# Feed-forward weights at other distances from their moving operand, and three raw weight buffers instead of four

## The chip, the cores and the metric

The kernel runs on one core of one Trainium2 chip. The metric is the device time of one execution in microseconds. The engines are TensorE (PE, with its weight loads shown apart as PEld), VectorE (DVE), ScalarE (ACT), GpSimd (POOL) and SyncE (SP, which here issues the weight DMAs).

## The reference

A trunk of four residual layers over 256 tokens of width 1024, in float32. Each layer adds a token mixer (layer 0 and 3 a Mamba-2 SSD, layer 1 an HGRN2 recurrence, layer 2 a gated DeltaNet), then cross-attention into 256 memory tokens, then a gated feed-forward block; a final RMSNorm follows. The part that the change is about:

```python
D_MODEL = 1024; SEQ = 256; DEPTH = 4; D_FF = 2816
...
def conv_glu_ffn(h, up_w, conv_w, conv_b, down_w):
    gate, up = jnp.split(h @ up_w, 2, axis=-1)
    gate = causal_dwconv(gate, conv_w) + conv_b
    return (jax.nn.silu(gate) * up) @ down_w
...
    for i in range(DEPTH):
        hn = rmsnorm(x, ln_mix[i])
        # mixer i % 3: mamba2, hgrn2, gated_deltanet
        x = x + mix
        x = x + memory_cross_attention(rmsnorm(x, ln_xattn[i]), rmsnorm(mem, ln_mem[i]), xa_q[i], xa_kv[i], xa_o[i])
        x = x + conv_glu_ffn(rmsnorm(x, ln_ffn[i]), f_up[i], f_conv_w[i], f_conv_b[i], f_down[i])
    return rmsnorm(x, final_norm)
```

## The kernel before

All activations stay on the chip with the feature on the partition and the 256 tokens along the row. Every weight matrix streams in once, in tiles of 128 x 1024 float32 (512 KB). `prep` (L152) makes one such tile ready: a DMA on SP's queue fills `raw`, ScalarE casts it to the rounded format float32r as `wH` (L160), VectorE subtracts the two to get the rest `wL` (L161). There are four `raw`, three `wH` and three `wL` buffers. `mm3` (L166) then multiplies in three matmuls: wH by the activations' high part (L168), wH by their low part (L169), wL by the high part (L170). In all of them the weights' 128 x 128 block is the stationary operand, loaded by an LDWEIGHTS before its matmul, and 256 columns of activations are the moving one; only in `proj_tok` and in the second half of `mem_kv` is it the other way round.

`proj` (L229) uses one weight tile for 8 k-tiles x 3 matmuls; its moving operand is `hH` or `hL`. `out_proj` (L254) walks groups of four k-tiles and uses a tile for 2 column blocks x 4 k-tiles x 3; its moving operand is `aH` or `aL`. `ffn` (L453) calls `proj` 22 times with two tiles each (`f_up`, 1056 matmuls a layer, into `ffps`), and then `out_proj` for `f_down` (528 matmuls a layer, into `acc`), which has 22 k-tiles in six groups. `mem_kv` before the next layer's mixer has 384 matmuls.

The order of work is the scheduler's: weight tiles are made under a raised priority, so they run as far ahead as buffers allow, and `Weave` mixes the steps of the mixers' heads in between the weight matmuls. Each engine and SP's queue take their instructions in order.

Addresses matter for what follows. In the built program a partition's row of SBUF holds `hH` from byte 20672, `hL` from 28864, `wH` from 80896, 84992 and 89088, `wL` from 93184, 97280 and 101376, `aH` and `aL` from 105664 to 120000 in steps of 2048, and `mH` and `mL` (the split memory tokens) from 131264 and 139456. All `hH`, `hL`, `aH`, `aL`, `mH`, `mL` rows begin 192 bytes past a multiple of 512, all `wH` and `wL` rows on one, and the blocks within a tile are multiples of 512 bytes apart. So between a moving operand and the weights that are loaded meanwhile the distance, moving minus stationary, is 192 bytes modulo 512 (320 where the roles are exchanged). A few others exist: in the attention scores keys move and queries stand, both 192 past a multiple, so the distance is 0; the Mamba dt projection has 32 columns of weights for each k-tile, so its weights start 128 bytes further each time.

Of the kernel before, what the change touches and what calls it, by code (L numbers as in the profile page):

```python
# [9 lines left out]
F32R = mybir.dt.float32r  # L10
# [6 lines left out]
P = 128  # L17
D = 1024
T = 256
# [3 lines left out]
NFF = 22  # L23
# [63 lines left out]
def tile_trunk(ctx: ExitStack, tc: tile.TileContext, io: dict, out: bass.AP, layers=range(DEPTH), parts="mxf", final=True):  # L87
    nc = tc.nc
    ACT, DVE, POOL, PE = nc.scalar, nc.vector, nc.gpsimd, nc.tensor
    weave = Weave()  # L90
    WB = [4,3,3]
    HL = [607, 282, 1973, 470, 14335, 1000]
    NL = [9214]
    LAT = [21000, 5620, 1450, 1042, 1588, 1117, 1724, 2353, 942, 2058, 8335, 1093, 4452, 2125, 1556]
# [6 lines left out]
    wp = ctx.enter_context(tc.tile_pool(name="wp", bufs=3))  # L101
# [6 lines left out]
    def phase(name, bufs=1):  # L108
        return tc.tile_pool(name=name, bufs=bufs, reuse_waits="tile")
# [4 lines left out]
    def bank(name):  # L114
        return ps_acc.tile([P, 512], F32, tag="acc", name=name)

    def flat(ap):
        return ap.rearrange("p a b -> p (a b)")

    def pcol(name, i):  # L120
        o = PO[name] + i
        return prm[:, o:o + 1]

    def f32(ap):
        return ap.bitcast(F32)
# [23 lines left out]

    between = []  # L150

    def prep(src, n=1024, step=1024):  # L152
        with tc.high_priority(offset=PRIO):
            raw = wp.tile([P, 1024], F32, tag="raw", name="raw", bufs=WB[0])
            H = wp.tile([P, 1024], F32R, tag="wH", name="wH", bufs=WB[1])
            L = wp.tile([P, 1024], F32R, tag="wL", name="wL", bufs=WB[2])
            for o in range(0, n, step):
                c = slice(o, min(n, o + step))
                nc.sync.dma_start(out=raw[:, c], in_=src[:, c])
                ACT.copy(H[:, c], raw[:, c])  # L160
                DVE.tensor_tensor(out=L[:, c], in0=raw[:, c], in1=f32(H[:, c]), op=ALU.subtract)  # L161
                if len(between) > 1:
                    between[-1](between.pop(0))
        return H, L

    def mm3(dst, aH, aL, bH, bL, start, stop):  # L166

        PE.matmul(dst, aH, bH, start=start, stop=False, skip_group_check=True)  # L168
        PE.matmul(dst, aH, bL, start=False, stop=False, skip_group_check=True)  # L169
        PE.matmul(dst, aL, bH, start=False, stop=stop, skip_group_check=True)  # L170

    def split(src, H, L):
        return (ACT.copy(H, src), DVE.tensor_tensor(out=L, in0=src, in1=f32(H), op=ALU.subtract))  # L173

# [5 lines left out]

    def split_gain(src, g, H, L):

        ACT.activation(out=H, in_=src, func=AF.Copy, scale=g)  # L183
        DVE.scalar_tensor_tensor(out=L, in0=src, scalar=g, in1=f32(H), op0=ALU.mult, op1=ALU.subtract)  # L184


    def exp_ln_tables(*after):

        i = ACT.preload_act_table_set("natural_log_exp_and_others")
        behind([i] * len(after), after)  # L190
# [35 lines left out]
        yield 440, 0  # L226


    def proj(srcs, ps):  # L229

        for i, s in enumerate(srcs):
            H, L = prep(s)
            for kt in range(KT):
                c = slice(kt * P, (kt + 1) * P)
                mm3(ps[:, i * T:(i + 1) * T], H[:, c], L[:, c], hH[:, kt, :], hL[:, kt, :],
                    i == 0 and kt == 0, kt == KT - 1)
                if kt % 2:
                    weave.tick(654)
# [12 lines left out]
                    if k % 2:  # L251
                        weave.tick(654)

    def out_proj(wsrc, nk, a, gens=None, gname=None, layer=0, last=False):  # L254


        accs = [bank(f"acc{b}") for b in range(4)]
        ng = (nk + 3) // 4
        st = Stats(DVE if last else POOL)
        for g in range(ng):  # L260
            n = min(4, nk - 4 * g)
            if gens is not None:
                weave.finish(gens[g])
            aH, aL = [], []
            for k in range(0, n, 2):
                H = ap_.tile([P, 2, T], F32R, tag="aH", name="aH")
                L = ap_.tile([P, 2, T], F32R, tag="aL", name="aL")
                split(a[:, 4 * g + k:4 * g + k + 2, :], H, L)
                aH += [H[:, 0, :], H[:, 1, :]]
                aL += [L[:, 0, :], L[:, 1, :]]  # L270
            for b in range(4):
                H, L = prep(wsrc[g, b], n * T)
                for cb in range(2):
                    for k in range(n):
                        kt = 4 * g + k
                        c = slice(k * T + cb * P, k * T + (cb + 1) * P)
                        mm3(accs[b][:, cb * T:(cb + 1) * T], H[:, c], L[:, c], aH[k], aL[k],
                            kt == 0 and cb == 0, kt == nk - 1)
                        if k % 2:
                            weave.tick(654)  # L280
                if g == ng - 1:
                    xs = flat(xT[:, 2 * b:2 * b + 2, :])
                    DVE.tensor_tensor(out=xs, in0=xs, in1=accs[b], op=ALU.add)
                    if gname is not None:
                        for kt in (2 * b, 2 * b + 1):
                            split_gain(xT[:, kt, :], pcol(gname, layer * 8 + kt), hH[:, kt, :], hL[:, kt, :])
                    st.add(xs)
                    if last:
                        for kt in (2 * b, 2 * b + 1):
                            fg = pcol("final", kt)  # L290
                            if b < 3:
                                POOL.tensor_scalar(out=KTt[:, kt, :], in0=xT[:, kt, :], scalar1=fg, scalar2=None, op0=ALU.mult)
                            else:
                                ACT.activation(out=KTt[:, kt, :], in_=xT[:, kt, :], func=AF.Copy, scale=fg)
        return st

    def conv(c, src, wcol, width, bias):

        if bias is None:
            ACT.activation(out=c, in_=src, func=AF.Copy, scale=wcol(width - 1))  # L300
        else:
            ACT.activation(out=c, in_=src, func=AF.Identity, scale=wcol(width - 1), bias=bias)
        for j in range(1, width):
            DVE.scalar_tensor_tensor(out=c[:, j:], in0=src[:, :T - j], scalar=wcol(width - 1 - j), in1=c[:, j:],
                                     op0=ALU.mult, op1=ALU.add)
# [80 lines left out]
    def attention(layer, st):  # L386
        with ExitStack() as ex:
# [46 lines left out]
            for h in range(4):  # L434
# [12 lines left out]
                if h < 3:  # L447
                    behind(split(KTt[:, 2 * h + 2:2 * h + 4, :], *kvs[h + 1][0]), sp)
                gens.append(weave.push(late(AL[2], head(h, qH, qL))))
            return out_proj(io["xa_o"][layer], KT, oT, [gens[:2], gens[2:]], "ln_ffn" if "f" in parts else None, layer)  # L450

    def late(ns, gen):
# [4 lines left out]
    def ffn(layer, st, hook=None, last=False):  # L457
        with ExitStack() as ex:
            wk = ex.enter_context(phase(f"ff{layer}", 2))
            aT = wk.tile([P, NFF, T], F32, name="aT", bufs=1)  # L460
            rs = np_.tile([P, T], F32, tag="nrs", name="nrs", bufs=1)
            def gate(t, ps):
                gu = wk.tile([P, 2, T], F32, tag="gu", name="gu")
                DVE.tensor_tensor(out=gu, in0=ps.rearrange("p (a b) -> p a b", a=2),
                                  in1=rs.unsqueeze(1).to_broadcast([P, 2, T]), op=ALU.mult)
                c = wk.tile([P, T], F32, tag="c", name="c")
                conv(c, gu[:, 0, :], lambda j: pcol("f_cw", (layer * NFF + t) * 3 + j), 3, pcol("f_cb", layer * NFF + t))
                silu = ACT.activation(out=c, in_=c, func=AF.Silu)
                DVE.tensor_tensor(out=aT[:, t, :], in0=c, in1=gu[:, 1, :], op=ALU.mult)
                return silu  # L470

            todo = []
            for t in range(NFF):
                ps = bank("ffps")
                proj([io["f_up"][layer, 2 * t + i] for i in range(2)], ps)
                todo.append((t, ps))
                if t == 0:
                    continue
                if t == 1:
                    st.rs(rs)  # L480
                for u in todo:
                    silu = gate(*u)
                todo = []
                if t == 6 and hook is not None:
                    hook(silu)
            exp_ln_tables(silu)
            return out_proj(io["f_down"][layer], NFF, aT, last=last)

    def softplus(u, n, tmp):

# [669 lines left out]
    for i, l in enumerate(layers):  # L1160
# [7 lines left out]
        else:  # L1168
            for kt in range(KT):
                g = "ln_xattn" if "x" in parts else "ln_ffn"  # L1170
# [13 lines left out]
    for b in range(4):  # L1184
        o = Vt.rearrange("p a (b t) -> p (a b) t", t=T)[:, 2 * b:2 * b + 2, :]
# [125 lines left out]
```

## Time and profile before

| | us |
|---|---|
| median of two runs (2066.68 and 2073.19) | 2069.93 |
| the profiled execution | 2072.47 |
| its span, first to last instruction | 2070.7 |
| TensorE busy in it | 2025.5 |
| VectorE busy | 1590.6 |
| ScalarE busy | 1282.5 |
| mean granted TensorE clock, share of full | 0.997 |

A matmul is counted as busy from its start to a modelled end, and the next one starts before that end. So the busy time says that TensorE hardly stops, and the time of one matmul is read from start to start.

### The profile page before, as it was taken

To read this page: it belongs to the slowest core of one execution; us is meant where nothing else is said; L and a number is where in the kernel's file an instruction comes from. 1 tells how busy PE (TensorE), PEld (TensorE's weight loads), DVE (VectorE), ACT (ScalarE), POOL (GpSimd) and SP (SyncE) were. 2 spreads that over 40 slices of the span, in tenths; PEclk is the share of its full clock that TensorE was granted. 3 is DMA by queue.
4 is the path that set the end of the run, shared out by engine and by line. 5 is a ranking of instruction groups with operands and counts; after the bars stand their busy time and mean duration, and the time that the engine had idled before them with its cause. 6 is when DMAs were issued, how large, how long until landed. Compare 5 with 4: busy or idle time off the path is not lost.

```text
span 2070.7 us, 42162 instructions
## 1 busy us (share of the span) xinstructions
PE 2025.5 (98%) x17084; PEld 1971.5 (95%) x17084; DVE 1590.6 (77%) x2423; ACT 1282.5 (62%) x1874; POOL 344.5 (17%) x468
## 2 busy tenths in 40 slices
PE   8999999999999999999999999999999999999997
PEld 8999999999999899999988889999999999999997
DVE  6899787875688777866786775778757999778765
ACT  6677666654565566555676875666545777666553
POOL 2032211000132110001064451110000223201001
PEclk9999999999999999999999999999999999999999
DMA  7554555655654446666543333456656444545663
GB/s 239 163 155 152 162 154 162 206 188 170 206 157 140 149 137 195 203 195 192 186 130 126 114 113 115 139 163 211 195 179 196 151 154 150 174 133 183 186 189 115
DMA packets 110372, 343.10 MB, mean 166 GB/s; under 512 B 15456, under 2 KB 25312, under 8 KB 110176
## 3 DMA queue, kind: packets, MB, share of 16 engines
q1 hardware_dynamic: 106176, 333.42, 52.0%
q10 hardware_dynamic: 3744, 6.71, 1.0%
q8 instruction: 134, 2.20, 0.4%
q0 software_dynamic: 256, 0.26, 0.1%
q14 instruction: 62, 0.51, 0.1%
HBM read 336.42 MB, written 3.93 MB: 164 GB/s over the span
## 4 chain that ended last, share of the span: by engine, by line
PE 79%; DVE 6%; issue 5%; ACT 4%; DMA 3%; POOL 2%; ACTq 0%; SPq 0%; DVEq 0%; POOLq 0%
PE acc L168 7%; PE ffps L170 7%; PE acc L169 7%; PE ffps L169 7%; PE ffps L168 7%; PE acc L170 7%; PE mps L168 4%; PE mps L169 4%; PE mps L170 4%; DVE wL L161 2%; PE kvps L170 2%; PE kvps L168 2%; PE kvps L169 2%; PE qps L170 2%; PE qps L168 2%
## 5 line engine op out<-in xcount | busy, mean ns | idle before, releaser
L161 DVE TENSOR_TENSOR wL<-raw,wH 128x1024 fp32r<-128x1024 f32 (+2 forms) x639 | 776.1, 1216 | 318.9 <-ACT wH L160 316.6
L160 ACT CAST wH<-raw 128x1024 fp32r<-128x1024 f32 (+2 forms) x639 | 658.4, 1031 | 510.6 <-PE ffps L169 156.4
L168 PE MATMUL acc<-aH,wH 128*128 128x256 f32 x1408 | 396.4, 282 | 0.6 <-ACT aH L173 0.6
L170 PE MATMUL ffps<-hH,wL 128*128 128x256 f32 x1408 | 392.6, 279 | 1.8 <-DVE wL L161 1.7
L168 PE MATMUL ffps<-hH,wH 128*128 128x256 f32 x1408 | 392.0, 279 | 2.5 <-ACT hH L183 2.5
L170 PE MATMUL acc<-aH,wL 128*128 128x256 f32 x1408 | 393.0, 279 | 0.0
L169 PE MATMUL acc<-aL,wH 128*128 128x256 f32 x1408 | 392.4, 279 | 0.1
L169 PE MATMUL ffps<-hL,wH 128*128 128x256 f32 x1408 | 392.1, 279 | 0.2
L168 PEld LDWEIGHTS ffps<-hH,wH 128*128 128x128 f32 x1408 | 265.5, 189 | 3.4 <-ACT hH L183 3.3
L168 PEld LDWEIGHTS acc<-aH,wH 128*128 128x128 f32 x1408 | 265.2, 189 | 3.5 <-issue 1.3
L170 PEld LDWEIGHTS ffps<-hH,wL 128*128 128x128 f32 x1408 | 264.4, 188 | 4.1 <-DVE wL L161 3.7
L169 PEld LDWEIGHTS acc<-aL,wH 128*128 128x128 f32 x1408 | 265.6, 189 | 1.5 <-issue 0.5
L169 PEld LDWEIGHTS ffps<-hL,wH 128*128 128x128 f32 x1408 | 265.1, 188 | 1.1 <-DVE hL L184 0.6
L170 PEld LDWEIGHTS acc<-aH,wL 128*128 128x128 f32 x1408 | 264.6, 188 | 0.4 <-DVE wL L161 0.2
L168 PE MATMUL mps<-hH,wH 128*128 128x256 f32 x768 | 219.8, 286 | 0.0
L170 PE MATMUL mps<-hH,wL 128*128 128x256 f32 x768 | 215.0, 280 | 0.0
L169 PE MATMUL mps<-hL,wH 128*128 128x256 f32 x768 | 214.9, 280 | 0.0
L203 POOL TENSOR_TENSOR ns<-nsq 128x256 f32<-128x256 f32 x13 | 10.5, 811 | 856.5 <-ACT nsq L200 856.5
L168 PEld LDWEIGHTS mps<-hH,wH 128*128 128x128 f32 x768 | 145.1, 189 | 2.7 <-issue 2.4
L170 PEld LDWEIGHTS mps<-hH,wL 128*128 128x128 f32 x768 | 145.4, 189 | 0.1
L169 PEld LDWEIGHTS mps<-hL,wH 128*128 128x128 f32 x768 | 144.5, 188 | 0.3
L170 PE MATMUL gps<-hH,wL 128*128 128x256 f32 x448 | 127.2, 284 | 0.9 <-DVE wL L161 0.9
(397 smaller groups left out, 4489.9 us busy)
## 6 DMA issues: line engine op xcount, KB each, us to landing
raw<-f_up SPq DMA_DIRECT2D x176, 512.0 KB, 3.6
raw<-m_in SPq DMA_DIRECT2D x96, 512.0 KB, 3.5
raw<-f_down SPq DMA_DIRECT2D x80, 512.0 KB, 3.5
raw<-xa_kv SPq DMA_DIRECT2D x60, 512.0 KB, 4.2
raw<-g_in SPq DMA_DIRECT2D x48, 512.0 KB, 3.9
raw<-m_out SPq DMA_DIRECT2D x32, 512.0 KB, 3.5
raw<-xa_q SPq DMA_DIRECT2D x32, 512.0 KB, 3.5
raw<-xa_o SPq DMA_DIRECT2D x32, 512.0 KB, 3.5
```

The source lines that it names most:

```text
L160: ACT.copy(H[:, c], raw[:, c])
L161: DVE.tensor_tensor(out=L[:, c], in0=raw[:, c], in1=f32(H[:, c]), op=ALU.subtract)
L168: PE.matmul(dst, aH, bH, start=start, stop=False, skip_group_check=True)
L169: PE.matmul(dst, aH, bL, start=False, stop=False, skip_group_check=True)
L170: PE.matmul(dst, aL, bH, start=False, stop=stop, skip_group_check=True)
L203: self.eng.tensor_tensor(out=self.sum, in0=sq[:, :T], in1=sq[:, T:], op=ALU.add)
```

## The change

`prep` takes a parameter `far`, the distance in bytes modulo 512 from the weights to their moving operand. Its `wH` and `wL` buffers are 1152 instead of 1024 columns wide, and the tile uses 1024 of them from an offset of (192 - far) modulo 512 bytes. All callers keep 192, except the feed-forward block: f_up has one distance for its first eleven `proj` calls and another for the last eleven, f_down one for its first three groups (288 matmuls) and another for the last three (240), and both tables differ by layer. To make room for the six wider buffers, `raw` has three buffers instead of four.

```diff
-    WB = [4,3,3]
+    WB = [3,3,3]
...
-    def prep(src, n=1024, step=1024):
+
+    FAR = 192
+    UP = [(64, 96), (224, 256), (384, 416), (128, 288)]
+    DOWN = [(128, 160), (288, 352), (448, 192), (256, 384)]
+
+    def prep(src, n=1024, step=1024, far=FAR):
+        o = (FAR - far) % 512 // 4
         with tc.high_priority(offset=PRIO):
             raw = wp.tile([P, 1024], F32, tag="raw", name="raw", bufs=WB[0])
-            H = wp.tile([P, 1024], F32R, tag="wH", name="wH", bufs=WB[1])
-            L = wp.tile([P, 1024], F32R, tag="wL", name="wL", bufs=WB[2])
+            H = wp.tile([P, 1152], F32R, tag="wH", name="wH", bufs=WB[1])[:, o:o + 1024]
+            L = wp.tile([P, 1152], F32R, tag="wL", name="wL", bufs=WB[2])[:, o:o + 1024]
...
-    def proj(srcs, ps):
+    def proj(srcs, ps, far=FAR):
...
-            H, L = prep(s)
+            H, L = prep(s, far=far)
...
-    def out_proj(wsrc, nk, a, gens=None, gname=None, layer=0, last=False):
+    def out_proj(wsrc, nk, a, gens=None, gname=None, layer=0, last=False, fars=(FAR, FAR)):
...
-                H, L = prep(wsrc[g, b], n * T)
+                H, L = prep(wsrc[g, b], n * T, far=fars[2 * g // ng])
...
-                proj([io["f_up"][layer, 2 * t + i] for i in range(2)], ps)
+                proj([io["f_up"][layer, 2 * t + i] for i in range(2)], ps, UP[layer][2 * t // NFF])
...
-            return out_proj(io["f_down"][layer], NFF, aT, last=last)
+            return out_proj(io["f_down"][layer], NFF, aT, last=last, fars=DOWN[layer])
```

TensorE's instructions in the feed-forward layers stand in the same order before and after. With one raw buffer fewer the scheduler moves some others: single casts, subtractions and residual sums at the end of two of the f_down's, and many steps in layer 2's mixer. On SP's queue, in the first heads of layer 2's mixer (`raw<-g_in` are weight tiles; `gd<-MT`, `blk<-gd` and `U<-gd` carry a head's matrix out to memory and back), there stood before:

```order
L159 DMA raw<-g_in 128x1024
L928 DMA blk<-gd_12483 32x16x16
L159 DMA raw<-g_in 128x1024 x4
L958 DMA U<-gd_12485 128x4x128
L159 DMA raw<-g_in 128x1024
L927 DMA gd_12484<-MT 128x4x128
L928 DMA blk<-gd_12484 32x16x16
L159 DMA raw<-g_in 128x1024 x3
```

and now (the lines are six higher):

```order
L165 DMA raw<-g_in 128x1024
L934 DMA blk<-gd_12483 32x16x16
L165 DMA raw<-g_in 128x1024 x3
L964 DMA U<-gd_12485 128x4x128
L165 DMA raw<-g_in 128x1024
L933 DMA gd_12484<-MT 128x4x128
L165 DMA raw<-g_in 128x1024
L934 DMA blk<-gd_12484 32x16x16
L165 DMA raw<-g_in 128x1024 x3
```

Three weight tiles instead of four stand between the first head's `blk` and its `U`, and the one left over stands between the second head's `gd` and `blk`.

On VectorE, in the same heads (`kq`, `kd`, `gqd`, `MT` and `gatt` are steps of a head, `gc` the convolution that empties a weight product's bank `gps`), there stood before:

```order
L889 TENSOR_TENSOR kq<-qk,grs 128x2x128
L890 SCALAR_TENSOR_TENSOR kq<-qk,grs 128x2x128
L946 TENSOR_TENSOR kd<-er,kq 128x256
L947 TENSOR_TENSOR gqd<-er,kq 128x256
L919 SCALAR_TENSOR_TENSOR MT<-E,gtcol,gp 128x128 x3
L304 SCALAR_TENSOR_TENSOR gc_12853<-gps,prm,gc_12853 128x255
L919 SCALAR_TENSOR_TENSOR MT<-E,gtcol,gp 128x128
L304 SCALAR_TENSOR_TENSOR gc_12853<-gps,prm,gc_12853 128x254
L161 TENSOR_TENSOR wL<-raw,wH 128x1024
L304 SCALAR_TENSOR_TENSOR gc_12853<-gps,prm,gc_12853 128x253
```

and now:

```order
L895 TENSOR_TENSOR kq<-qk,grs 128x2x128
L896 SCALAR_TENSOR_TENSOR kq<-qk,grs 128x2x128
L310 SCALAR_TENSOR_TENSOR gc_12853<-gps,prm,gc_12853 128x255
L952 TENSOR_TENSOR kd<-er,kq 128x256
L310 SCALAR_TENSOR_TENSOR gc_12853<-gps,prm,gc_12853 128x254
L925 SCALAR_TENSOR_TENSOR MT<-E,gtcol,gp 128x128
L310 SCALAR_TENSOR_TENSOR gc_12853<-gps,prm,gc_12853 128x253
L925 SCALAR_TENSOR_TENSOR MT<-E,gtcol,gp 128x128 x3
L167 TENSOR_TENSOR wL<-raw,wH 128x1024
```

The three steps of the convolution now stand ahead of most of `MT`, and `gqd` comes later.

## Rows read from the trace of the kernel before

**Rows 1.** The page: the span, TensorE's busy time and count, and the engines' shares of the chain that ended last.

```profile
span 2070.7 us, 42162 instructions
...
PE 2025.5 (98%) x17084; PEld 1971.5 (95%) x17084; DVE 1590.6 (77%) x2423; ACT 1282.5 (62%) x1874; POOL 344.5 (17%) x468
...
PE 79%; DVE 6%; issue 5%; ACT 4%; DMA 3%; POOL 2%; ACTq 0%; SPq 0%; DVEq 0%; POOLq 0%
```

**Rows 2.** The waits of TensorE, longest first in total: who waited for whom, us in total, times, longest.

```profile
PE kvps L168 <- ACT wH L160: 7.0, 1, 7.0
PE grp L1035 <- ACT S L1030: 3.6, 2, 1.8
...
PE ffps L170 <- DVE wL L161: 1.7, 5, 0.5
...
PE gps L170 <- DVE wL L161: 0.9, 2, 0.6
```

**Rows 3.** Windows in the feed-forward layers, TensorE alone: the window (us from the start of the span), its length, TensorE's busy time and the matmuls that touch the window, the granted clock, the DMA engines' share, GB/s. In order: layer 0 first half of f_up, then second half with f_down; layers 1 and 2 the same; layer 3 from the first half of f_up to the end of f_down.

```profile
348.00:385.00 37.00, 37.00 (x329) 1.00 0.65 208
400.00:519.00 119.00, 119.00 (x1013) 1.00 0.59 185
785.00:820.00 35.00, 35.00 (x312) 1.00 0.65 205
835.00:951.00 116.00, 116.00 (x1026) 1.00 0.65 192
1383.00:1420.00 37.00, 37.00 (x328) 1.00 0.65 206
1433.00:1549.00 116.00, 116.00 (x1026) 1.00 0.62 192
1886.00:2058.00 172.00, 172.00 (x1462) 1.00 0.56 172
```

**Rows 4.** Groups by line in two of these windows, 835 to 951 us (first row) and 1886 to 2058 us (second): busy us and mean ns of one, idle before.

```profile
L169 PE MATMUL ffps<-hL,wH 128*128 128x256 f32 x171 | 47.2, 276 | 0.0
...
L169 PE MATMUL ffps<-hL,wH 128*128 128x256 f32 x315 | 88.5, 281 | 0.0
```

**Rows 5.** TensorE in order of time around 396 us, in layer 0's f_up: start us, duration us, line and names.

```profile
395.52 0.28 PE L168 MATMUL ffps<-hH,wH 128*128 128x256 f32 x1
395.63 0.28 PE L169 MATMUL ffps<-hL,wH 128*128 128x256 f32 x1
396.37 0.39 PE L170 MATMUL ffps<-hH,wL 128*128 128x256 f32 x1 [0.45 <-DVE wL L161]
...
396.94 0.28 PE L168 MATMUL ffps<-hH,wH 128*128 128x256 f32 x1
```

**Rows 6.** The page's costliest groups: of f_up's matmuls the first and the last of three lines.

```profile
L170 PE MATMUL ffps<-hH,wL 128*128 128x256 f32 x1408 | 392.6, 279 | 1.8 <-DVE wL L161 1.7
...
L169 PE MATMUL ffps<-hL,wH 128*128 128x256 f32 x1408 | 392.1, 279 | 0.2
```

**Rows 7.** TensorE in order of time in the attention scores of layer 1's second head: the first two and the last of twelve matmuls in a row.

```profile
729.62 0.28 PE L168 MATMUL sc<-k1H,qH 128*128 128x256 f32 x1
729.74 0.28 PE L169 MATMUL sc<-k1L,qH 128*128 128x256 f32 x1
...
730.94 0.28 PE L170 MATMUL sc<-k1H,qL 128*128 128x256 f32 x1
```

**Rows 8.** Windows in mem_kv of layer 1 and of layer 2, TensorE alone, columns as in rows 3.

```profile
535.00:564.00 29.00, 29.00 (x248) 1.00 0.61 182
970.00:994.00 24.00, 24.00 (x214) 1.00 0.60 183
```

**Rows 9.** TensorE in order of time in layer 0's dt projection: the first and the last of eighteen matmuls in a row.

```profile
57.32 0.28 PE L168 MATMUL dtps<-hH,wH 128*32 128x256 f32 x1
...
59.25 0.28 PE L170 MATMUL dtps<-hH,wL 128*32 128x256 f32 x1
```

**Rows 10.** Making weight tiles in layer 1's f_up: DMA issues (count, KB each, median us to landing), then SP's queue, VectorE and ScalarE in order of time.

```profile
raw<-f_up SPq DMA_DIRECT2D x176, 512.0 KB, 3.6
...
843.80 16.53 SPq L159 DMA_DIRECT2D raw<-f_up  x7
...
842.56 1.22 DVE L161 TENSOR_TENSOR wL<-raw,wH 128x1024 fp32r<-128x1024 f32 x1
...
844.07 1.05 ACT L160 CAST wH<-raw 128x1024 fp32r<-128x1024 f32 x1 [0.92 <-PE ffps L169]
...
852.23 1.05 ACT L160 CAST wH<-raw 128x1024 fp32r<-128x1024 f32 x1 [1.17 <-PE ffps L169]
```

**Rows 11.** Layer 2's mixer in order of time: SP's queue, ScalarE, TensorE.

```profile
1062.99 2.16 SPq L159 DMA_DIRECT2D raw<-g_in  x3
1081.31 0.38 SPq L958 DMA_DIRECT2D U<-gd  x1
1081.79 0.45 SPq L159 DMA_DIRECT2D raw<-g_in  x1
...
1087.34 2.05 SPq L159 DMA_DIRECT2D raw<-g_in  x4
...
1086.10 1.04 ACT L160 CAST wH<-raw 128x1024 fp32r<-128x1024 f32 x1 [3.25 <-DMA raw<-g_in]
...
1087.41 0.36 ACT L1030 COPY S<-gs 128x256 f32<-128x256 f32 x1
...
1087.83 0.71 PE L1035 MATMUL grp<-S,kd 128*128 128x128 f32 x4 [1.82 <-ACT S L1030]
```

**Rows 12.** The window of layer 2's mixer with its output projection: length, busy us and instructions of TensorE, its weight loads, VectorE, ScalarE and GpSimd, clock, DMA share, GB/s.

```profile
999.00:1316.00 317.00, 301.72 (x2441) 284.18 (x2440) 235.18 (x441) 223.10 (x334) 121.88 (x271) 0.99 0.41 130
```

## The prediction, made before the changed kernel ran

> **What bounds the kernel now.** I read the page's first lines, then TensorE's waits, then the feed-forward stretches one by one. TensorE is busy 2025.5 of 2070.7 us, in 17084 matmuls, and holds 79% of the chain that ended last [rows 1]. The 45.2 us in which it is idle are many small waits: the longest, 7.0 us, is the start; behind it come waits of 2 to 4 us in total each, none on a weight tile in the feed-forward layers worth more than 2 us [rows 2]. So the time is the number of matmuls times the distance from one start to the next, and that step is what to look at.
>
> A row of the windows view counts every matmul that touches the window, so the step is (window + one duration) / count. In the feed-forward stretches with no wait it takes just two values [rows 3, 4]: (37 + 0.28)/329 = 113.3 ns in the first half of layer 0's f_up, 119.28/1013 = 117.8 ns from there to the end of its f_down; 113.3 ns in all of layer 1 and layer 2 (116.28/1026); 117.8 ns in all of layer 3 (172.28/1462). The duration moves with it, 276 against 281 ns. The granted clock is 1.00, the 2.4 GHz level, in all seven, so this is no clock effect. The program, the shapes and the 192 bytes are the same in all these stretches; what differs is how the stream started. At 396 us TensorE waits 0.45 us for wL, and the steps are 113 ns before and 118 ns after, up to 520 us [rows 3, 5]. I read that as a stream of moving reads and the load of the next weights getting in each other's way by one of two fixed amounts, set at each restart and kept until the next.
>
> **The change part by part.**
>
> *The distance.* f_up and f_down run 4 x (1056 + 528) = 6336 matmuls: 1408 on each of mm3's three lines for ffps, 4224 in all [rows 6], and 528 per layer in f_down (22 k-tiles x 8 column blocks x 3). No instruction is added or moved there; only the address of the stationary operand slides by up to 480 bytes. Before, 3696 of them (528 of layer 0, 1584 each of layers 1 and 2) step at 113.3 and 2640 at 117.8 ns: 418.8 + 311.0 = 729.8 us, a mean of 115.2 ns. After, fifteen of the sixteen sections have a distance that f_up and f_down have not had, so the cost is bounded from the nearest rows:
> - At 0 bytes (the attention scores, keys moving, queries stationary) eleven steps in a row from 729.62 to 730.94 us make 120 ns [rows 7]. All at 120 ns: 6336 x 4.8 ns = +30.4 us.
> - At 320 bytes (the second half of mem_kv, weights and activations with their roles exchanged, and the first half at 192) both values occur: 118.1 ns at 535 us, 113.4 ns at 970 us [rows 8]. So a distance need not choose between the two.
> - The small dt projection has 32 weight columns per k-tile, so its weights start 128 bytes further each time and the distance runs through 192, 64, 448 and 320. It steps at (59.25 - 57.32)/17 = 113.5 ns [rows 9]: the better value stands at four distances, and even a short weight load doesn't go under it. I take 113.3 ns for the floor. All there: 6336 x -1.9 ns = -12.0 us.
>
> I take the middle, 116.7 ns: distances such as 224, 288 and 352 lie next to the two whose rows show either value (mean 115.5), 64, 96, 416 and 448 between these and the 120 ns at zero. That is 6336 x 1.5 ns = **+9.5 us**, between -12 and +30.
>
> Here the Trainium skill speaks for another result. "TensorE: Matmul & The Clock Gate", Part 2 (step by step, LDWEIGHTS), says that TensorE reads SBUF through two independent ports, one for the moving operand and one for the weight load, and that loading the next weights takes no read bandwidth from the running matmul. By that the distance would be worth nothing, and the term 0. The trace doesn't bear it out fully: the step is 113.3, 117.8 or 120 ns for one shape at one clock [rows 3, 7].
>
> *Three raw buffers.* A weight tile's DMA is issued when VectorE has subtracted the tile four (now three) places ahead. In f_up seven issues take 16.5 us, 2.7 us apart, and each follows at once on a subtraction: it ends at 843.78, the DMA that refills the buffer goes at 843.80 and that tile is cast at 852.23 [rows 10], 8.4 us later. Landing takes 3.6 us in the median, so some 4.8 us are spare; with three buffers the issue moves one tile, 2.7 us, later, and about 2 us stay. ScalarE waits there for TensorE to release wH, not for the DMA [rows 10], and three wH tiles are 8 us of matmuls ahead. Cost there: 0. If that cover were gone, each late tile would cost its lateness, below 1 us.
>
> The place where it can cost is layer 2's mixer, the gated delta net. There SP's queue also carries the head's transfers: the DMA of U waits until 1081.31, and the raw tiles queued behind it go at 1081.79 and 1087.34, after three at 1063 [rows 11]. So what is loaded before such a block is all that TensorE has; ScalarE waits 3.25 us for a raw tile at 1086, the copy of S is queued behind that cast at 1087.41, and TensorE waits 1.82 us for S [rows 11]. The new order of SP's queue has one raw tile fewer ahead of U in the first head and takes the raw loads apart around blk later. For each of the eight heads one tile less is ready. There is room: for a weight tile itself TensorE waits in this stage 0.9 us in all, on two occasions [rows 2]. I bound the buffers' part by 0 and four heads that wait as this one did, 4 x 1.8 = 7 us. The scheduler also puts the conv steps of VectorE in another place among the head's steps; I bound that by a quarter, either way, of the 15.3 us for which TensorE idles in this stage (317 - 301.7) [rows 12], so -4 to +11 together. I take **+2 us**, about the one wait that a row shows.
>
> *The rest.* All other weights keep 192 bytes. Their streams may restart on the other value after a feed-forward layer; 384 matmuls of the next mem_kv are 1.7 us each way, and I take 0.
>
> *The sum.* The profiled execution took 2072.47 us (span 2070.7): 2072.5 + 9.5 + 2 = 2084. It lies 2.5 us over the median of the runs, 2069.93, so the forecast for the median is 2069.9 + 11.5 = **2081 us**.
>
> **The rivals.**
> 1. *The distance does nothing; each section falls on 113.3 or 117.8 by its restart.* For: the two values at one distance, and the skill's rule above. Against: 120 ns at zero [rows 7]. If the sections draw evenly, 115.5 ns, 6336 x 0.3 = +2, with the +2 of the buffers 2074 us; that all the sections that ran at 117.8 fall on it again gives 2072.
> 2. *192 is a poor place and most others sit on the floor.* For: layers 0 and 3 paid 117.8 for 2640 matmuls, and the dt projection ran at 113.5 through four distances. Against: with 32 columns its weight load is a quarter as long. It gives -12 + 2: 2060 us. More than 2% faster would need 108.7 ns a step, below anything that 256 columns with a weight load show here.
> 3. *Some distances make the weight load and the moving reads collide all the way, and 120 isn't the worst.* Place: those sections of f_up and f_down whose distance meets the delay between the two reads. It decides from a mean of 115.2 + 41.4/6.336 = 121.7 ns on. If half of the matmuls went at 130, 3168 x 14.8 = +47 us: 2119 us. For: zero bytes need not be the worst, since the two reads don't start together by anything the trace shows. Against: no stretch without a wait, at any distance in this trace, steps at more than 121 ns.
> 4. *The raw buffers starve TensorE.* If the spare 2 us were eaten, 272 feed-forward tiles would be late by under 1 us each, and the wH tiles hide that first; only if the delta-net waits all came, +9 on top of the +2 of the forecast, 2090 us: still no change by 2%.
>
> **How the numbers follow.** 2% of 2070 is 41 us, about what a measurement of this kernel can tell from no change. The forecast (a mean step between 115.7 and 120 ns, 2073 to 2110 us) gets 0.61, rival 1 0.14, rival 2 0.10, rival 3 0.10, rival 4 beside the others 0.05. Low end: -12 for the floor and -2 in the delta net, 2056. High end: +30 and +8 of the delta net's +11, 2108; beyond it lie rival 3 and little else. Faster by over 2% 0.02, within 0.87, slower 0.11 (rival 3, and a little of the forecast's upper end with the delta net).
>
> **What would show it.** In the windows of each half of f_up and f_down, the step should be one steady value per section, none under 113, most between 113.3 and 120; the same values for the two sections that share a distance (128, 256, 288, 384) would prove the distance, different ones rival 1. A section over 125 ns without waits is rival 3. ScalarE's waits for raw tiles should grow in the delta net alone. Wrong I would be if the mixers, whose distance stays, moved by more than 10 us.

## The result, and the profile after

The changed kernel takes 2090.77 us in the median of two runs (2089.07 and 2092.46) against 2069.93: a ratio of 1.0104, 95% interval 1.0073 to 1.0135. That is a loss of 1.0%, less than the 2% that one comparison can tell. The interval comes from two runs of each kernel and says little of the kernel before's own spread: in the later comparisons its 43 runs lie between 2057.24 and 2083.09 us, all below both runs here. So the loss is there, but its size is less sure than the interval says. The profiled execution took 2092.46 us. Its page, against [rows 1]:

```profile
span 2090.7 us, 42161 instructions
...
PE 2044.1 (98%) x17084; PEld 1991.0 (95%) x17084; DVE 1590.3 (76%) x2423; ACT 1282.5 (61%) x1875; POOL 342.5 (16%) x468
...
PE 85%; issue 5%; DVE 5%; ACT 4%; DMA 1%; POOL 1%; DVEq 0%; ACTq 0%; SPq 0%; POOLq 0%
```

TensorE is busy 18.6 us longer with the same 17084 matmuls; the span is 20.0 us longer. So on balance the time went into longer steps; TensorE's waits grew in one stage and shrank in others. The windows of the sixteen sections, TensorE alone, columns as in [rows 3], in the order first and second half of f_up, first and second half of f_down, layers 0 to 3:

```profile
348.00:385.00 37.00, 37.00 (x316) 1.00 0.63 201
400.00:455.00 55.00, 55.00 (x461) 1.00 0.62 194
464.00:491.00 27.00, 27.00 (x229) 1.00 0.58 181
497.00:519.00 22.00, 22.00 (x187) 1.00 0.48 149
790.00:820.00 30.00, 30.00 (x256) 1.00 0.57 179
845.00:897.00 52.00, 52.00 (x436) 1.00 0.62 193
905.00:933.00 28.00, 28.00 (x242) 1.00 0.59 189
938.00:960.00 22.00, 22.00 (x186) 1.00 0.47 143
1400.00:1440.00 40.00, 40.00 (x340) 1.00 0.60 194
1450.00:1505.00 55.00, 55.00 (x472) 1.00 0.64 200
1511.00:1538.00 27.00, 27.00 (x241) 1.00 0.60 194
1543.00:1565.00 22.00, 22.00 (x197) 1.00 0.48 156
1905.00:1950.00 45.00, 45.00 (x378) 1.00 0.58 182
1957.00:2012.00 55.00, 55.00 (x474) 1.00 0.59 188
2018.00:2047.00 29.00, 29.00 (x244) 1.00 0.58 184
2053.00:2075.00 22.00, 22.00 (x187) 1.00 0.37 120
```

By the prediction's formula, (window + 0.28)/count, each row gives its section's step, to about 0.5 ns for the short ones. The table is sharper: it has the mean step over all starts of TensorE in the section that follow one another without a wait.

| layer | f_up 1 | f_up 2 | f_down 1 | f_down 2 |
|---|---|---|---|---|
| 0 | 64: 117.6 ns | 96: 120.0 | 128: 118.7 | 160: 118.7 |
| 1 | 224: 118.3 | 256: 120.0 | 288: 116.7 | 352: 120.0 |
| 2 | 384: 118.7 | 416: 117.3 | 448: 113.4 | 192: 113.3 |
| 3 | 128: 119.8 | 288: 116.7 | 256: 120.0 | 384: 118.7 |

The clock is 1.00, 2.4 GHz, in every row, as before. Weighted by its matmuls the table gives 748.7 us, 118.2 ns a step, where [rows 3] gave 729.8.

By the starts of the stages, from one stage's first matmul to the next one's, f_up gained 2.4, 4.7, 3.5 and 0.4 us in layers 0 to 3 and f_down (the last one with the final norm) 0.5, 2.6, 0.0 and 1.3: +15.4 in the feed-forward. Layer 2's mixer gained 4.5; the other stages come to 0.1 together, with +1.7 and -1.6 in the attention of layers 1 and 2 among them. The stages show 3.5 us less than the 18.9 of the steps, because waits shrank: TensorE's 1.7 us for wL in f_up [rows 2] are gone, which fits longer steps that give VectorE more time. The rest was not traced to a wait.

In layer 2's mixer the window that answers to [rows 12], all engines:

```profile
1010.50:1332.00 321.50, 302.35 (x2455) 284.85 (x2454) 236.98 (x442) 224.60 (x337) 119.72 (x271) 0.98 0.42 129
```

TensorE idles 321.5 - 302.35 = 19.2 us instead of 15.3. Its wait for gsq in this window, and ScalarE's for raw tiles, first in the kernel before and then in the changed one, where the first is TensorE's longest:

```profile
PE l L883 <- ACT gsq L880: 0.7, 2, 0.4
...
ACT wH L160 <- DMA raw<-g_in: 6.5, 2, 3.3
```

```profile
PE l L889 <- ACT gsq L886: 8.9, 2, 8.7
...
ACT wH L166 <- DMA raw<-g_in: 12.3, 3, 8.8
```

The wait for gsq, a ScalarE step of a head, grew from 0.7 to 8.9 us. The one for S, 3.6 us in [rows 2], is gone, and others have shrunk: so 8.2 us more of this wait made only 3.9 us more idle time. Where it comes from, in order of time, SP's queue and then ScalarE, beside [rows 11]:

```profile
1051.91 4.83 SPq L165 DMA_DIRECT2D raw<-g_in  x3
1069.83 0.38 SPq L964 DMA_DIRECT2D U<-gd  x1
1070.30 0.46 SPq L165 DMA_DIRECT2D raw<-g_in  x1
...
1075.95 1.04 ACT L166 CAST wH<-raw 128x1024 fp32r<-128x1024 f32 x1 [8.77 <-DMA raw<-g_in]
...
1078.84 0.63 ACT L886 ACTIVATE gsq<-qk 128x512 f32<-128x512 f32 x1
```

SP's queue stands at the head's U until 1069.83. The raw tile behind it goes at 1070.30 and lands some 5.6 us later. ScalarE's cast waits 8.77 us for it, and gsq, which needs no weight, is queued behind that cast.

The wait has a tail. Two windows of TensorE alone, the wait and the time soon after it, and the first and last of nine matmuls in a row in the second:

```profile
1071.00:1079.50 8.50, 0.00 (x0) 0.71 0.76 224
1082.50:1085.00 2.50, 2.50 (x14) 0.53 0.00 0
```

```profile
1082.89 0.41 PE L174 MATMUL gps<-hH,wH 128*128 128x256 f32 x1
...
1084.59 0.40 PE L176 MATMUL gps<-hH,wL 128*128 128x256 f32 x1
```

While TensorE waits, its granted clock falls from 1.00 to 0.50, the 1.2 GHz level, and it is back at 1.00 only at some 1084.8 us: these matmuls step at (1084.59 - 1082.89)/8 = 212 ns instead of 113 to 118.

### The profile page after: what moved, and what is told of

It is laid out like the page before. It is cut to its first block, busy times and chain, and to the rows that moved or that the text cites. A ratio compares the mean times of both kernels' runs of the same rounds, so it can differ in the third digit from the quotient of the medians.

```text
span 2090.7 us, 42161 instructions
## 1 busy us (share of the span) xinstructions
PE 2044.1 (98%) x17084; PEld 1991.0 (95%) x17084; DVE 1590.3 (76%) x2423; ACT 1282.5 (61%) x1875; POOL 342.5 (16%) x468
## 4 chain that ended last, share of the span: by engine, by line
PE 85%; issue 5%; DVE 5%; ACT 4%; DMA 1%; POOL 1%; DVEq 0%; ACTq 0%; SPq 0%; POOLq 0%
PE ffps L176 8%; PE ffps L174 8%; PE ffps L175 8%; PE acc L174 7%; PE acc L175 7%; PE acc L176 7%; PE mps L174 4%; PE mps L175 3%; PE mps L176 3%; PE kvps L176 2%; PE kvps L174 2%; PE kvps L175 2%; DVE wL L167 2%; PE qps L176 2%; PE qps L175 2%
## 5 line engine op out<-in xcount | busy, mean ns | idle before, releaser
L174 PE MATMUL ffps<-hH,wH 128*128 128x256 f32 x1408 | 396.5, 282 | 2.5 <-ACT hH L189 2.5
L175 PE MATMUL ffps<-hL,wH 128*128 128x256 f32 x1408 | 396.6, 282 | 0.1
```

## The experiments

Two things were to be settled: whether the distance itself sets the step, or each section merely draws a value when its stream restarts (when TensorE takes up its matmuls again after a wait); and whether the mixer pays for the missing raw buffer. In e1 to e4, e6 and e7 the diffs are against the changed kernel, in e5, e8 and e9 against the kernel before.

**e1: three raw buffers, everything at 192.**

```diff
-    UP = [(64, 96), (224, 256), (384, 416), (128, 288)]
-    DOWN = [(128, 160), (288, 352), (448, 192), (256, 384)]
+    UP = [(192, 192), (192, 192), (192, 192), (192, 192)]
+    DOWN = [(192, 192), (192, 192), (192, 192), (192, 192)]
```

> The changed kernel with every distance back at 192: three raw buffers and the wider wH and wL alone. If the distances made the feed-forward layers slower, each of the sixteen halves steps at 113.3 or 117.8 ns as before, and only layer 2's mixer keeps its +4.5 us: 2069.9 + 5 = 2075 us, give or take 4 for the value on which each stream restarts. If the fewer raw buffers or the wider tiles made them slower (the rival), the time stays near 2090 and f_up steps above 118 ns.

Measured: 2076.12 us in the median of ten runs, ratio 1.0028 (0.9994 to 1.0063). The runs lie between 2062.63 and 2090.68. The profiled one took 2067.93; its windows of layer 1 and layer 2, second half of f_up with f_down:

```profile
830.00:943.00 113.00, 113.00 (x999) 1.00 0.63 190
1435.00:1550.00 115.00, 115.00 (x979) 1.00 0.59 183
```

113.4 and 117.8 ns; layers 0 and 3 are at the first as well. In the kernel before it was layer 3 and most of layer 0 that had the higher value [rows 3]. So which layer is dear at 192 is no property of the layer. The mixer gained 3.7 us over before.

**e2: the feed-forward at 448,** for 448 and 192 were the only sections at the floor.

```diff
-    UP = [(64, 96), (224, 256), (384, 416), (128, 288)]
-    DOWN = [(128, 160), (288, 352), (448, 192), (256, 384)]
+    UP = [(448, 448), (448, 448), (448, 448), (448, 448)]
+    DOWN = [(448, 448), (448, 448), (448, 448), (448, 448)]
```

> All of f_up and f_down at 448, the one new distance that stepped at 113.4 ns (layer 2, first half of f_down). If the distance alone sets the step: 113.3 ns in all sixteen halves, 6336 x -1.9 ns = -12 us against the kernel before, +5 for layer 2's mixer: 2063 us. If 448 has two values like 192 and layer 2's restart happened to give the lower one (the rival): 113.3 and 117.8 ns mixed, 2070 to 2080 us.

Measured: 2080.53 us in the median of ten runs (2066.26 to 2090.67), ratio 1.0033 (1.0001 to 1.0065). The same windows of layers 1 and 2:

```profile
835.00:949.00 114.00, 114.00 (x971) 1.00 0.59 183
1436.00:1549.00 113.00, 113.00 (x1000) 1.00 0.63 190
```

117.7 and 113.3 ns: 448 has the same two values as 192. The idea that 448 alone gives the floor falls.

**e3: the feed-forward at 256.**

```diff
-    UP = [(64, 96), (224, 256), (384, 416), (128, 288)]
-    DOWN = [(128, 160), (288, 352), (448, 192), (256, 384)]
+    UP = [(256, 256), (256, 256), (256, 256), (256, 256)]
+    DOWN = [(256, 256), (256, 256), (256, 256), (256, 256)]
```

> All of f_up and f_down at 256, which stepped at 120.0 ns in two places of the changed kernel (layer 1, second half of f_up; layer 3, first half of f_down). If the distance sets the step: 120 ns in all sixteen halves, 6336 x 4.8 ns = +30 us, with +5 for layer 2's mixer 2105 us. If the restart sets it and the distance doesn't (the rival): a mixture of steps and a time like that of the changed kernel or of the one with 192, 2075 to 2090 us.

Measured: 2105.37 us in the median of four runs, ratio 1.0165 (1.0126 to 1.0205). Layer 0's window, second half of f_up with f_down:

```profile
402.00:524.00 122.00, 122.00 (x1019) 1.00 0.59 181
```

122.28/1019 = 120.0 ns, and the same in all sixteen sections. Between e1 and e3 only the distance differs, so distance alone is worth 29 us of the median here. The four runs of e3 lie within 3.4 us, the ten each of e1 and e2 within 28 and 24, the nineteen of the kernel before in the same comparison within 21. That points to the two values of 192 and 448 in the feed-forward as the source of most of the spread: all sections on the one or on the other make a difference of 6336 x 4.4 ns = 28 us.

**e4: the distances dealt out to other sections,** none but 384 where it was in the changed kernel, and 0, 32, 320 and 480 for the first time in the feed-forward.

```diff
-    UP = [(64, 96), (224, 256), (384, 416), (128, 288)]
-    DOWN = [(128, 160), (288, 352), (448, 192), (256, 384)]
+    UP = [(0, 32), (320, 480), (448, 64), (224, 96)]
+    DOWN = [(192, 448), (256, 288), (352, 160), (416, 384)]
```

> The distances dealt to other halves and layers, and four that had not stood in f_up or f_down: f_up 0, 32 | 320, 480 | 448, 64 | 224, 96; f_down 192, 448 | 256, 288 | 352, 160 | 416, 384. If the step belongs to the distance, it goes along with it: 96, 256 and 352 at 120.0 ns, 160 and 384 at 118.7, 224 at 118.3, 64 at 117.6, 416 at 117.3, 288 at 116.7, 448 at 113.3. If it belongs to the place in the program or to the restart, the values stay where they were. If in addition the pattern repeats every 256 bytes, 0 steps like 256 (120.0), 32 like 288 (116.7), 480 like 224 (118.3) and 320 like 64 (117.6).

Measured: 2089.51 us in a single run. Windows of 0 and 32 (layer 0's f_up), 320 and 480 (layer 1's), and 96 (layer 3):

```profile
350.00:395.00 45.00, 45.00 (x378) 1.00 0.63 199
403.00:458.00 55.00, 55.00 (x474) 1.00 0.64 194
...
780.00:820.00 40.00, 40.00 (x341) 1.00 0.65 206
840.00:892.00 52.00, 52.00 (x442) 1.00 0.63 193
...
1955.00:2010.00 55.00, 55.00 (x461) 1.00 0.58 183
```

The steps from all starts:

| distance | changed kernel | e4 | the distance 256 bytes off, e4 |
|---|---|---|---|
| 96 / 352 | 120.0 / 120.0 | 120.0 / 120.0 | |
| 256 | 120.0, 120.0 | 120.0 | 0: 119.9 |
| 224 | 118.3 | 118.3 | 480: 118.3 |
| 128 / 384 | 118.7, 119.8 / 118.7, 118.7 | - / 118.6 | |
| 160 / 416 | 118.7 / 117.3 | 117.3 / 118.7 | |
| 288 | 116.7, 116.7 | 117.8 | 32: 116.7 |
| 64 | 117.6 | 117.8 | 320: 117.6 |
| 448 / 192 | 113.4 / 113.3 | 113.3, 117.6 / 113.4 | |

The value goes with the distance and not with the layer, and distances 256 bytes apart agree, to within the two values that some have. Only 192 and 448 show the floor of 113.3 here; 160 and 416, 288 and 128 have two values as well, closer together.

**e5: the kernel before with three raw buffers and its narrow tiles.**

```diff
-    WB = [4,3,3]
+    WB = [3,3,3]
```

> The kernel before with three raw buffers and nothing else: wH and wL as narrow as before, no distances. If the number of raw buffers costs what layer 2's mixer lost (307.3 to 311.8 us from the end of mem_kv to the start of attention), that stage takes 311 to 312 us here, with one wait of some 8 us of ScalarE for a weight tile of g_in and one of TensorE for gsq behind it. If the wider wH and wL cost it (the rival), it takes 307 us. The feed-forward halves step at 113.3 or 117.8 ns, by the restart.

Measured: 2067.25 us in a single run, beside 2068.61 of the kernel before; fifteen of the sixteen sections had drawn 113.3 ns, so the total says nothing of the buffers. The mixer does: 313.3 us, +6.1. Its waits, TensorE and ScalarE:

```profile
PE l L883 <- ACT gsq L880: 6.9, 1, 6.9
...
ACT wH L160 <- DMA raw<-g_in: 10.5, 5, 7.1
```

The wait for gsq is there without wide tiles and without other distances. It comes from the missing buffer, together with the order that the scheduler makes with three: e5 has both, and no run holds the one and changes the other.

**e6: 192, with one tile in four at another distance.** A table gives each half of each layer's feed-forward one odd distance: 32 and 96, 352 and 160, 224 and 416, 288 and 0.

```diff
-    UP = [(64, 96), (224, 256), (384, 416), (128, 288)]
-    DOWN = [(128, 160), (288, 352), (448, 192), (256, 384)]
+    KICK = [(32, 96), (352, 160), (224, 416), (288, 0)]
+
+    def kicked(layer, half, n):
+        return FAR if n % 4 else KICK[layer][half]
...
```

> The feed-forward weights at 192, but every fourth tile at another distance, one for each half: layer 0 32 and 96, layer 1 352 and 160, layer 2 224 and 416, layer 3 288 and 0. If the step at 192 is a state that only a restart of the stream sets, the three tiles after each such tile keep the value they had before it. If a change of distance can set it too, the value after it differs from the one before it in some cases; a distance after which it is always 113.3 ns would hold the feed-forward layers at (24 x 117 + 72 x 113.3)/96 = 114.2 ns, 6 us under the 115.2 of the profiled execution before. The time is between 2062 and 2085 us either way.

Measured: 2076.53 us in a single run. Windows of a tile at 96 and the three at 192 behind it, then of a tile at 0 and the three behind it:

```profile
402.05:404.85 2.80, 2.80 (x26) 1.00 0.77 199
405.00:413.00 8.00, 8.00 (x73) 1.00 0.70 217
1945.05:1947.85 2.80, 2.80 (x26) 1.00 0.57 190
1948.00:1956.00 8.00, 8.00 (x70) 1.00 0.62 194
```

Both odd tiles step at 120 ns by their starts (the window is too short to give it to better than 4%); behind the first, 192 runs at 8.28/73 = 113.4 ns, behind the second at 8.28/70 = 118.3 (117.8 by all 72 starts). This was so each time: the lower value after every tile at 96, 352, 160, 224 and 416 (8 or 9 of each), the higher after all 8 at 0. After 32 and 288 the first two of a layer left 117.7, the later ones 113.3. So a change of distance sets the value, without any restart.

**e7: the changed kernel, with U fetched by GpSimd's queue,** to free the raw tiles that stand behind it on SP's.

```diff
-                nc.sync.dma_start(out=U, in_=rows(d1))
+                nc.gpsimd.dma_start(out=U, in_=rows(d1))
```

> The changed kernel with the DMA of U, for which SP's queue waits in layer 2's mixer, issued from GpSimd's queue, so that the raw weight tiles don't stand behind it. If that blocked queue with one raw buffer fewer is what costs the mixer its 4.5 us, ScalarE's waits for raw tiles of g_in there fall from 12.3 us to under 4, the 8.7 us wait of TensorE for gsq goes, and the stage from the end of mem_kv to the start of attention takes 300 to 308 us instead of 311.8. If it is the other order of VectorE's steps (the rival), the stage stays at 311 to 312 us. GpSimd waits for U's source itself, which may hold back the next head's substitution. The feed-forward halves step as in the changed kernel.

Measured: 2097.34 us in a single run; the mixer took 316.0 us, 4.2 more than in the changed kernel. TensorE's longest wait and ScalarE's for raw tiles:

```profile
PE tps L970 <- DMA U<-gd: 11.7, 4, 4.3
...
ACT wH L166 <- DMA raw<-g_in: 3.2, 1, 3.2
```

The raw tiles did come free, 12.3 us of waits became 3.2, and the wait for gsq went. But U itself now comes late, four times, 11.7 us in all. The expected gain, a stage of 300 to 308 us, did not come, and 316.0 is not the 311 to 312 of its rival either (that the other order of VectorE's steps is the cause): one wait took the place of another. So e7 agrees with gsq having waited for the raw tile, and leaves open what the stage would take with the tiles free and U on time.

**e8 and e9: the kernel before, with some of its matmuls off 192 throughout.** If a change of distance can bring the lower value back, a few matmuls in each tile should keep 192 there. The first k-tile of `hH` is laid 32 bytes (e8) or 96 bytes (e9) ahead of its place, so that its two matmuls of the 24 on a weight tile run at 160 or 96.

```diff
+class Gap:
+
+    def __init__(self, tile, gap):
+        self.tile, self.gap = tile, gap
+
+    def __getitem__(self, key):
+        _, kt, c = key
+        o = kt * T + (self.gap if kt else 0)
+        return self.tile[:, o + (c.start or 0):o + (T if c.stop is None else c.stop)]
...
-    hH = cst.tile([P, KT, T], F32R, name="hH")
+    hH = Gap(cst.tile([P, KT * T + 8], F32R, name="hH"), 8)
```

> The kernel before (four raw buffers, narrow tiles) with 32 free bytes between the first k-tile of hH and the rest: everything stays at 192, only the first k-tile of hH has 160 to its weights, so two or three of every 24 matmuls of proj stand at the distance after which the stream stepped at 113.3 ns eight times out of eight. If so few matmuls set the state: f_up of all layers and the product of the Mamba input step at 113.3 ns in every tile past the first k-tile (about 114 over a tile), the time is about 2069 - 10 = 2059 us and the runs lie closer together than the 2060 to 2082 us of the kernel before. If a whole tile at the other distance is needed (the rival): 113.3 and 117.8 ns mixed as before, 2065 to 2075 us with the same spread.

Measured: 2062.30 us in the median of twelve runs (2058.50 to 2067.57) against 2074.19 of the kernel before in the same comparison (2057.24 to 2083.09): ratio 0.9952 (0.9929 to 0.9975). It is faster than the kernel before, by less than 2% but with an interval clear of 1, and its runs lie within 9 us instead of 26. Its second half of f_up and its f_down in layers 0 and 1:

```profile
400.00:452.00 52.00, 52.00 (x456) 1.00 0.65 200
458.00:513.00 55.00, 55.00 (x488) 1.00 0.57 178
835.00:884.00 49.00, 49.00 (x430) 1.00 0.64 200
890.00:945.00 55.00, 55.00 (x488) 1.00 0.58 177
```

114.6 ns with the two odd matmuls counted in, and 113.3 in f_down, which inherits the value from f_up; layers 2 and 3 are the same. This one profile would show little by itself, as e5 drew the lower value in fifteen sections with no gap; the twelve runs carry it. e9 has 24 floats of gap instead of 8:

```diff
-    hH = Gap(cst.tile([P, KT * T + 8], F32R, name="hH"), 8)
+    hH = Gap(cst.tile([P, KT * T + 24], F32R, name="hH"), 24)
```

> The same with 96 free bytes: the first k-tile of hH has 96 to its weights, another distance after which the stream always stepped at 113.3 ns. If the state can be set from any such distance, this is the same as with 32 bytes, within 4 us. If few matmuls don't do it or 96 does it only as a whole tile: 2065 to 2075 us.

Measured: 2067.24 us in the median of ten runs (2061.90 to 2069.37), ratio 0.9966 (0.9941 to 0.9991). Layer 1's second half of f_up fell on the higher value and stayed there to the end of f_down, while the other sections ran at the lower one:

```profile
835.00:885.00 50.00, 50.00 (x427) 1.00 0.63 199
892.00:950.00 58.00, 58.00 (x494) 1.00 0.56 173
```

117.8 and 118.0 ns. A whole tile at 96 set the lower value every time (e6), two matmuls of it do not always.

The two runs also settle a rival that e1 to e6 leave: there only the weights slide, so their own address might set the step, and not the distance. In the built programs of e8 and e9 everything behind `hH` begins 32 and 96 bytes later, `wH` from byte 80928 and 80992. So in f_down the weights start 32 and 96 bytes past a multiple of 512, with the distance still 192, and the steps are 113.3 ns (e8) and 113.3 or 117.8 (e9). The changed kernel's weights began at the same 32 and 96 bytes past a multiple in its sections at 160 and 96, which stepped at 118.7 and 120.0 ns. The step goes with the distance.

## Why the prediction was right, and where its terms were not

The time, 2090.8, lies in the range of 2056 to 2108, on the forecast's side and within 2%. The sum was 8 to 9 us short: +11.5 forecast, +20.8 measured by the medians, +20.0 by the spans. That 20.0 is itself partly luck: it depends on which value the kernel before drew in its sections, and in that profile 3696 of the 6336 matmuls had the lower one.

**The distance, +9.5 forecast, +15.4 measured.** The mechanism held: the step depends on the distance (e3, e4), each section ran at one mean value, sections that share a distance agree at 256, 288 and 384 to 0.1 ns and at 128 to 1.1, none is below 113.3, and the 120 ns at zero, read from eleven steps [rows 7], was the ceiling. The step that failed is the middle, 116.7 ns; it was 118.2, and by that alone 6336 x 1.5 = 9.5 us more. It rested on neighbours: 224, 288 and 352 were taken as 115.5 because they lie beside 192 and 320. They ran at 118.3, 116.7 and 120.0. Nearness in bytes means little; what repeats is the distance modulo 256. Seen so, the two values at 320 in [rows 8] stood for 64 as well, and the 120 ns at zero for 256 rather than for the far end of a slope. The matmul part of the range, -12 to +30, was right because both its ends were rows: e3 at 256 throughout came out at 120.0 ns, as the upper end had it.

A smaller miss: the term left out that slower matmuls shorten waits, which gave back some 3 us.

**Rival 1, the distance does nothing,** is refuted by e3 and e4. For this kernel so is what it took from the Trainium skill ("TensorE: Matmul & The Clock Gate", Part 2, step by step, LDWEIGHTS), that loading the next weights takes no read bandwidth from the running matmul: by that e1 and e3 would take the same time, and they differ by up to 6.7 ns in each step. Whether the two ports or something behind them cause it, no run shows. What it had right is that at 192 there is a draw, and at 448 too (e2). **Rival 2** had the floor right and its breadth wrong: in the changed kernel only 448 and 192 reached it. Its point against itself, that a weight load of 32 columns is a quarter as long, is not what the profile of the kernel before has: 108 ns for those of the dt projection, 189 for those of f_up. **Rival 3** did not occur: no section ran above 120.0 ns.

**The raw buffers, +2 forecast, +4.5 measured.** The place and the chain of causes were as forecast: raw tiles behind U on SP's queue, a cast that waits, work for TensorE queued behind the cast. What was late was gsq rather than S, for 8.7 us rather than 1.8 [rows 11], and about half of it was taken from other waits; the bound of +11 covers it. e5 shows that the buffer, with the order that follows from it, and not the tile width causes it. The same stage in the other runs says how sharp these numbers are: with three buffers +3.7 (e1, e3), +6.1 (e5), +7.0 (e6), with four +0.4 and +2.3 (e8, e9). Part of that may be the two values of its own matmuls at 192. The time for which TensorE idles from the stage's first matmul to the first of the attention parts the two better: 13.7, 14.2 and 14.4 us with four buffers (before, e8, e9), 16.6 to 19.1 in the eight runs with three. That the feed-forward pays nothing for the buffer was right, but not that ScalarE's waits for raw tiles grow in the delta net alone. Two more rows of the changed kernel's waits:

```profile
ACT wH L166 <- DMA raw<-xa_kv: 16.7, 17, 3.3
...
ACT wH L166 <- DMA raw<-f_up: 0.4, 2, 0.2
```

In mem_kv, where before it was 0.2 us in all, they add up to 16.7. TensorE did not feel it: the three mem_kv stages between layers kept their times (45.7, 44.0 and 44.0 us) to 0.1 us.

**"Set at each restart and kept until the next"** [rows 5] was half right. A restart can set the value, but so does a change of distance (e6), and e8 makes use of it. The prediction also took the profiled 2072.5 as a steady base, where the kernel before lies between 2057 and 2083 us; the forecast's 2.5 us between profile and median are within that.

Open: why a restart gives one value or the other, why 32 and 288 set either, and what in the reads makes 0 and 96 dearest. A version with four raw buffers and the changed distances was not tried, since the wide tiles leave no room for the fourth.

## What to carry to other kernels

When TensorE is never idle, divide windows by their matmul counts: steps that differ at one clock and one shape point at where operands lie, and a single reading of a few addresses is a poor base for interpolating between them; measure the ends and take the range from them. When runs of one program spread by a per cent, see whether its sections step at two values before trusting a difference of that size; here laying one k-tile 32 bytes off narrowed the spread from 26 to 9 us and gained 0.5%. A prefetch buffer is worth what the longest block in its queue makes of it, so look for its cost where the queue carries waiting transfers, not where most of the tiles are.

## What the runs showed of the hardware

For float32r matmuls of 256 columns, each with its own 128 x 128 weight load, at 2.4 GHz throughout, the step depends on the distance between moving and stationary rows modulo 256 bytes, as far as the multiples of 32 bytes that ran show it: 113.3 or 117.7 ns at 64 and 192, 116.7 or 117.8 at 32, 117.3 or 118.7 at 160, 118.3 at 224, 118.7 or 119.8 at 128, 120.0 at 0 and 96. At 64 the lower value was seen only as 320, in the kernel before [rows 8].

The two values at 192 are states that hold over hundreds of matmuls. They change at some restarts and at changes of distance: in e6 a tile at 96, 160, 224, 352 or 416 always left the lower one behind it, a tile at 0 always the higher. Runs of one kernel with the feed-forward at 192 or 448 lie within 21 to 28 us of some 2070, the four with it at 256, which has one value only, within 3.4 us (e3).
